# A two-layer hybrid encoder trunk on one core: order of the matmuls in a feature tile, shared PSUM slots, a scan in four parts

## The chip, the cores and the metric

The kernel runs on one core of a Trainium2 chip. The metric is the device time of one execution in microseconds (us), taken as the median of several runs; lower is better. The engines are called TensorE (PE; PEld is its weight load), VectorE (DVE), ScalarE (ACT), GpSimd (POOL) and SyncE (SP), as in the profile.

## The reference, cut to what matters

Two layers work on `x`, 256 tokens of 1024 features, in float32. Each has a token-mixing part and an MLP.

```python
h = rms_norm(x, norm_mix_pre[l])
zq, zk, zv, zx, zy, zxq, zg = in_projection(h, w_in[l])
y_attn = diff_attention(rope(zq), rope(zk), zv, ...)      # 8 heads, two score maps each, chunk-causal
xc = causal_conv(zx, conv_w[l], conv_b[l])
y_lru = rg_lru(xc, ...) * gelu(zy)                        # h_t = a_t * h_(t-1) + u_t along the tokens
y_mem = memory_attention(zxq, mem, ...)                   # 4 heads over 256 memory tokens
merged = gate0 * (y_attn @ w_proj_attn) + gate1 * (y_lru @ w_proj_lru) + gate2 * (y_mem @ w_proj_mem)
x = x + rms_norm(merged @ w_out[l], norm_mix_post[l])
a = relu(rms_norm(x, norm_mlp_pre[l]) @ w_mlp_up[l])
x = x + rms_norm((a * a) @ w_mlp_down[l], norm_mlp_post[l])
```

## The kernel before

**Products in three terms.** Every large product is made from operands split in two parts, a high part (fp32r, the rounded value) and a low part (what is left). The weights come from HBM in chunks of 1 MB (`issue_dma`, three buffers `raw`). `issue_split` (lines 170 to 182) makes of each half chunk a tile `wh` on ScalarE (the cast of line 179) and a tile `wl` on VectorE (the subtraction of line 181); there are five buffers of each, and `weights` (line 184) keeps the splits five halves ahead of their use.

**Feature tiles.** `mm_feat` (line 236) computes 256 output features for all 256 tokens: two halves of 128 features, each in its own PSUM bank of a two-bank slot `acc`. In each half, for each of eight parts k of the contraction, there is one 512-column matmul with `wh` (line 247; its moving operand is two separate blocks of 256 columns, the high and the low part of the activations) and one 256-column matmul with `wl` (line 248), one after the other:

```python
for k in range(8):
    pe.matmul(o.rearrange("p (s n) -> p s n", s=2), wh[:, k, :], av[:, :, k, :], start=(k == 0), stop=False)
    state["mm"] = pe.matmul(o[:, 0:256], wl[:, k, :], av[:, 0, k, :], start=False, stop=(k == 7))
```

Then ScalarE copies one part of the result to SBUF (line 252) and VectorE adds the other (line 253); the sum is the tile `z`. The slot is free after that.

**Token tiles.** `mm_tok` (line 256) makes products with tokens on the partitions, 128 tokens and 512 features to a bank. Both halves of the tokens share one two-bank slot (`acc_tok`, line 121). It uses 512-column matmuls alone (lines 264 to 266). With `apart`, which is set for the last chunk of the second column half of wo and of the down product, all matmuls of token half 0 come ahead of those of half 1. `post_half` and `post_end` (lines 362 and 376) then square the result on ScalarE (line 367, with the sum in `ss4`), multiply it by the gain on VectorE (lines 371 and 387), and add it, scaled, to the residual `xt` (line 388).

**PSUM.** `psacc` has two slots of two banks, `pssc` one slot of two banks for the attention scores (`sc`, line 114), and `psat` two slots of one bank for everything small (`at`).

**Side jobs.** The memory attention (`xattn`), the recurrent branch (`lru`) and the differential attention (`attn`) are generators. `tick`, called in the middle of and after each product tile, moves a job on by one step (`lru` by one step in two ticks), and what the step issues on TensorE is queued behind the last matmul traced so far. `lru` ends with one scan over 2048 columns (line 626) and four steps that make the pair tile `ylr` (lines 631 and 632). `attn` makes in `scores` (line 662) the two score maps of a head in one `sc` tile, whose exponentials (line 680) are the last to read it.

**Order.** The Tile framework places each engine's instructions in an order of its own, by priorities and a time model; each engine then works in order. `tc.high_priority()` brings a block forward. In each layer follow: the memory query product, the recurrent input, the two gates of `lru`, q, k, v, then for each of three branches a gate and a projection (with `attn` beside them, from line 837), then wo, the up product and the down product. In layer 0 memory products for layer 1 stand behind wo and behind the down product; in layer 1 nothing does.

Of the kernel before, what the change touches and what calls it, by code (L numbers as in the profile page):

```python
# [9 lines left out]
F32 = mybir.dt.float32  # L10
# [3 lines left out]
ALU = mybir.AluOpType  # L14
# [54 lines left out]
def trunk(ctx, tc, x_in, xt_in, mem_in, memt_in, w_in, par_in, lamv_in, post_in, rope_in, out):  # L69
    nc = tc.nc  # L70
    act, dve, pe, pool = nc.scalar, nc.vector, nc.tensor, nc.gpsimd
# [4 lines left out]
    p_pair = ctx.enter_context(tc.tile_pool(name="pair", bufs=6))  # L76
    p_tmp = ctx.enter_context(tc.tile_pool(name="tmp", bufs=9))
    p_sm = ctx.enter_context(tc.tile_pool(name="sm", bufs=4))
    ps_acc = ctx.enter_context(tc.tile_pool(name="psacc", bufs=2, space=bass.MemoryType.PSUM))
    ps_sc = ctx.enter_context(tc.tile_pool(name="pssc", bufs=1, space=bass.MemoryType.PSUM))  # L80
    ps_at = ctx.enter_context(tc.tile_pool(name="psat", bufs=2, space=bass.MemoryType.PSUM))

    def pair(name):
# [9 lines left out]
    def hl(t):  # L93

        return t.rearrange("p (s k n) -> p s k n", s=2, k=8)
# [9 lines left out]
    def f8(t):  # L105
        return t.rearrange("p (k n) -> p k n", k=8)

    def tmp(name, dt=F32):
        return p_tmp.tile([128, 512], dt, tag="tmp", name=name)
# [2 lines left out]
        return p_sm.tile([128, n], F32, tag="sm_" + name, name=name)  # L112

    def sc():
        return ps_sc.tile([128, 1024], F32, tag="sc", name="sc")

    def acc():

        return ps_acc.tile([128, 2, 512], F32, tag="acc", name="acc")

    def acc_tok():
        a = acc()
        return [a[:, t, :] for t in range(2)]

# [111 lines left out]
    def mm_feat(key, a):  # L236

        ps = acc()
        av = hl(a)
        for j in range(2):
            wh, wl = (f8(t) for t in weights(*key, j))
            o = ps[:, j, :]
            for k in range(8):
                pe.matmul(o.rearrange("p (s n) -> p s n", s=2), wh[:, k, :], av[:, :, k, :], start=(k == 0), stop=False)  # L247
                state["mm"] = pe.matmul(o[:, 0:256], wl[:, k, :], av[:, 0, k, :], start=False, stop=(k == 7))  # L248
            if j == 0:
                tick()  # L250
        z = tmp("z")
        act.copy(two(z), ps[:, :, 256:512])  # L252
        dve.tensor_tensor(two(z), two(z), ps[:, :, 0:256], op=ALU.add)  # L253
        return z

    def mm_tok(pss, key, a_of, first, last, apart=False):
# [96 lines left out]
    def two(ap):  # L353
        return ap.rearrange("p (i n) -> p i n", i=2)
# [222 lines left out]
    def lru(l, xc, rgw, g2, done):  # L577
        wv = rgw.rearrange("p (c n d) -> p c n d", c=2, n=8)
        xv = f8(xc)
        av, tv = duo("lru")  # L580
        for j in range(4):
            sl = slice(j * 512, (j + 1) * 512)
            ti, xs = tv[:, sl], xc[:, sl]

            def gate(c):
                ps = at()
                for i in range(2):
                    f = 2 * j + i
                    pe.matmul(ps[:, i * 256:(i + 1) * 256], wv[:, c, f, :], xv[:, f, :], start=True, stop=True)
                return ps  # L590

            za, zi = gate(0), gate(1)
            for i in range(2):
                f = 2 * j + i
                act.activation(out=f8(tv)[:, f, :], in_=zi[:, i * 256:(i + 1) * 256], func=AF.Tanh, scale=0.5,
                               bias=hbi[:, l, f:f + 1])
            dve.scalar_tensor_tensor(ti, ti, 1.0, xs, op0=ALU.add, op1=ALU.mult)
            for i in range(2):
                f = 2 * j + i
                dve.tensor_scalar(f8(xc)[:, f, :], za[:, i * 256:(i + 1) * 256], par[:, l, P_BA, f:f + 1], -44.0,  # L600
                                  op0=ALU.add, op1=ALU.max)
            act.activation(out=xs, in_=xs, func=AF.Exp, scale=-1.0)
            yield
        act.activation(out=xc, in_=xc, func=AF.Ln, bias=1.0)
        yield
        for j in range(4):
            sl = slice(j * 512, (j + 1) * 512)
            a, xs = av[:, sl], xc[:, sl]
            act.activation(out=xs, in_=xs, func=AF.Exp, scale=-1.0)
            e = tmp("lE")  # L610
            for i in range(2):
                f = 2 * j + i
                act.activation(out=f8(av)[:, f, :], in_=f8(xc)[:, f, :], func=AF.Exp, scale=ncsp[:, l, f:f + 1])
                act.activation(out=e[:, i * 256:(i + 1) * 256], in_=f8(xc)[:, f, :], func=AF.Tanh,
                               scale=csp[:, l, f:f + 1])
            act.activation(out=xs, in_=a, func=AF.Square)
            dve.scalar_tensor_tensor(xs, xs, 1.0, e, op0=ALU.add, op1=ALU.mult)
            yield
        act.activation(out=xc, in_=xc, func=AF.Sqrt, scale=0.25)
        yield  # L620
        for j in range(4):
            sl = slice(j * 512, (j + 1) * 512)
            dve.tensor_tensor(tv[:, sl], tv[:, sl], xc[:, sl], op=ALU.mult)
        dve.memset(f8(av)[:, :, 0:1], 0.0)
        yield
        dve.tensor_tensor_scan(xc, av, tv, 0.0, op0=ALU.mult, op1=ALU.add)
        yield
        ylr = done["y"] = pair("ylr")
        for j in range(4):
            sl = slice(j * 512, (j + 1) * 512)  # L630
            dve.scalar_tensor_tensor(xc[:, sl], xc[:, sl], 0.5, g2[:, sl], op0=ALU.mult, op1=ALU.mult)
            split_to(hi(ylr)[:, sl], lo(ylr)[:, sl], xc[:, sl])
            yield
# [23 lines left out]
    def attn(l, qT, kT, va, done):  # L657
# [3 lines left out]

        def scores(h):
            pbs[h] = []
            ps = sc().rearrange("p (c n) -> p c n", c=2)
            for b in range(2):
                nk = 128 * (b + 1)
                sv = ps[:, :, 128 * b:128 * b + nk]
                for c in range(2):
                    cs = slice(64 * c, 64 * c + 64)
                    pe.matmul(sv[:, c, :], qv[cs, h, b * 128:(b + 1) * 128], kv[cs, h, 0:nk], start=True, stop=True)  # L670
            for b in range(2):
                nk = 128 * (b + 1)
                sv = ps[:, :, 128 * b:128 * b + nk]
                dve.memset(sv[0:64, :, nk - 64:nk], NEG_BIG)
                nm = sm("anm", 2)
                dve.tensor_reduce(nm, sv, axis=AX.X, op=ALU.max, negate=True)
                e = tmp("ae")
                ss = sm("as", 2)
                for c in range(2):
                    act.activation(out=e[:, c * nk:(c + 1) * nk], in_=sv[:, c, :], func=AF.Exp, bias=nm[:, c:c + 1],  # L680
                                   accum_out=ss[:, c:c + 1])
                r = sm("ar", 2)
                dve.reciprocal(r, ss)
                dve.tensor_scalar(e[:, nk:2 * nk], e[:, nk:2 * nk], r[:, 1:2], lam[:, l:l + 1], op0=ALU.mult,  # L684
                                  op1=ALU.mult)
                dve.scalar_tensor_tensor(e[:, 0:nk], e[:, 0:nk], r[:, 0:1], e[:, nk:2 * nk], op0=ALU.mult,
                                         op1=ALU.subtract)
                pbs[h].append(e)
# [101 lines left out]
    for l in range(DEPTH):  # L790
# [8 lines left out]
        for j in range(4):  # L799
            ps = mm_feat((l, "xq", j), hx)  # L800
            sl = slice(j * 512, (j + 1) * 512)
# [4 lines left out]
        xc, g2 = duo("xcg")  # L806
        for j in range(4):
            ps = mm_feat((l, "x", j), hx)
# [6 lines left out]
        for j in range(4):  # L815
            ps = mm_feat((l, "y", j), hx)
# [6 lines left out]
        for nm, scale, dst, r in (("q", 0.125, qT, rq), ("k", 1.0, kT, rk)):  # L823
            for j in range(4):
                ps = mm_feat((l, nm, j), hx)
# [3 lines left out]
        for n in range(2):  # L829
            pss = acc_tok()  # L830
# [7 lines left out]
        for b, pj, yb in ((2, "pm", {"y": ym}), (1, "pl", ylr), (0, "pa", ya)):  # L838
# [4 lines left out]
            for j in range(4):  # L843
                sl = slice(j * 512, (j + 1) * 512)
                ps = mm_feat((l, "g%d" % b, j), hx)
# [8 lines left out]
                ps = mm_feat((l, pj, j), yb["y"])  # L854
# [11 lines left out]
            mem_gained(l + 1)  # L866
        st = post_begin(l, 0)
        for n in range(2):
            pss = acc_tok()
            for c in range(2):  # L870
                if l + 1 == DEPTH and n == 1 and c == 1:
                    state["ahead"] = 3
                mm_tok(pss, (l, "wo", 2 * n + c), lambda k: parts(mp, 4 * c + k), c == 0, c == 1,
                       n == 1 and c == 1)
            post_half(st, n, pss)
# [16 lines left out]
        for j in range(16):  # L892
            ps = mm_feat((l, "up", j), hx)
# [5 lines left out]
            if j > 0:  # L899
                for i, p in pend:  # L900
# [3 lines left out]
                    sl = slice((i % 4) * 512, (i % 4 + 1) * 512)  # L904
# [1 line left out]
                pend = []  # L906
        st = post_begin(l, 1)
        for n in range(2):
            pss = acc_tok()
            for c in range(8):  # L910

                def a_of(k):
                    f = 4 * c + k
                    return parts(sqs[f // 8], f % 8)

                mm_tok(pss, (l, "dn", 8 * n + c), a_of, c == 0, c == 7, n == 1 and c == 7)
            post_half(st, n, pss)
        post_end(st, pss[1])
    for t in range(2):
        for n in range(2):  # L920
            sl = slice(n * 512, (n + 1) * 512)
# [95 lines left out]
```

## Time and profile before

| | |
|---|---|
| median of 3 runs | 1160.94 us (1160.4 to 1161.4) |
| the profiled execution, its own time | 1162.9 us |
| its span, first to last instruction | 1161.1 us |
| PE busy | 1122.5 us, 97% |
| PEld / DVE / ACT busy | 82% / 74% / 61% |
| mean granted TensorE clock | 0.989 |
| HBM read | 203.02 MB, 176 GB/s over the span |

A row of the trace gives the start and the duration of an instruction, its engine, its line in the kernel, the operation, the tiles it writes and reads, and its shapes; in brackets stands how long the engine was idle before it and what ended that. Matmuls are pipelined: one starts long before the one ahead has ended, so the distance of their starts is the time that each takes of the engine.

### The profile page before, as it was taken

The numbers are of one execution on the slowest core, as the hardware profiler recorded it, in microseconds if no ns is written. First come the engines' busy times: TensorE is split into PE (matmuls) and PEld (weight loads), VectorE is DVE, ScalarE is ACT, GpSimd is POOL, SyncE is SP. The second block draws the span as 40 slices with busy tenths as digits, with TensorE's granted clock in tenths as the row PEclk, the third lists the DMA queues.
The fourth block names the chain that finished last, engine by engine and source line by source line (L and its number), as shares of the span: only waits on it lengthen the run. The fifth ranks groups of instructions, "written<-read, shape, count | busy, mean of one in ns | idle before, by whom it ended". The sixth has DMA issues, their size and how long they took to land. (4 is left out here: it accounts for less than half of the span.)

```text
span 1161.1 us, 15842 instructions
## 1 busy us (share of the span) xinstructions
PE 1122.5 (97%) x6096; PEld 956.6 (82%) x6096; DVE 863.4 (74%) x1347; ACT 705.2 (61%) x1112; POOL 0.7 (0%) x6
## 2 busy tenths in 40 slices
PE   7999999999999999999999999998999997999996
PEld 5789888778888888888888888877788886888885
DVE  6979789778877687774457787987888666887453
ACT  6756695656556566663446667947665554766341
POOL 0000000000000000000000000000000000000000
PEclk9999999989999999999999999999999998999998
DMA  9655346644456545555554534665344553556550
GB/s 326 242 215 181 110 155 207 217 145 146 145 204 214 192 173 185 187 183 205 201 202 167 210 109 145 213 213 179 122 146 167 212 183 109 187 199 213 181 181 37
DMA packets 34779, 209.28 MB, mean 180 GB/s; under 512 B 3856, under 2 KB 8080, under 8 KB 10768
## 3 DMA queue, kind: packets, MB, share of 16 engines
q1 hardware_dynamic: 34128, 206.18, 50.5%
q10 hardware_dynamic: 576, 2.10, 0.5%
q8 instruction: 48, 0.79, 0.3%
q14 instruction: 27, 0.22, 0.1%
HBM read 203.02 MB, written 1.05 MB: 176 GB/s over the span
## 5 line engine op out<-in xcount | busy, mean ns | idle before, releaser
L181 DVE TENSOR_TENSOR wl<-raw,wh 128x1024 fp32r<-128x1024 f32 (+1 forms) x369 | 449.1, 1220 | 216.1 <-ACT wh L179 215.0
L179 ACT CAST wh<-raw 128x1024 fp32r<-128x1024 f32 (+1 forms) x369 | 385.0, 1048 | 325.8 <-PE acc L247 166.5
L247 PE MATMUL acc<-hx,wh 128*128 128x512 f32 x1536 | 550.3, 401 | 6.5 <-ACT vmg L835 2.9
L248 PE MATMUL acc<-hx,wl 128*128 128x256 f32 x1536 | 432.9, 282 | 0.0
L247 PEld LDWEIGHTS acc<-hx,wh 128*128 128x128 f32 x1536 | 290.1, 189 | 77.4 <-ACT vmg L835 3.7
L248 PEld LDWEIGHTS acc<-hx,wl 128*128 128x128 f32 x1536 | 292.0, 190 | 2.5 <-issue 2.0
L266 PE MATMUL acc<-wh,sq 128*128 128x512 f32 x256 | 99.6, 389 | 0.0
L265 PE MATMUL acc<-wl,sq 128*128 128x512 f32 x256 | 99.6, 389 | 0.0
L264 PE MATMUL acc<-wh,sq 128*128 128x512 f32 x256 | 99.6, 389 | 0.0
L253 DVE TENSOR_TENSOR z<-z,acc 128x512 f32<-128x512 f32 x128 | 87.1, 681 | 8.7 <-ACT z L252 8.7
L252 ACT COPY z<-acc 128x512 f32<-128x512 f32 x128 | 74.3, 580 | 9.5 <-PE acc L248 9.4
L265 PEld LDWEIGHTS acc<-wl,sq 128*128 128x128 f32 x256 | 48.1, 188 | 10.0
L264 PEld LDWEIGHTS acc<-wh,sq 128*128 128x128 f32 x256 | 48.1, 188 | 10.0
L266 PEld LDWEIGHTS acc<-wh,sq 128*128 128x128 f32 x256 | 48.1, 188 | 9.9
L247 PE MATMUL acc<-mh,wh 128*128 128x512 f32 x128 | 47.7, 412 | 6.9 <-ACT wh L179 6.9
L247 PE MATMUL acc<-xq,wh 128*128 128x512 f32 x128 | 46.5, 401 | 1.1 <-ACT wh L179 1.1
L247 PE MATMUL acc<-ylr,wh 128*128 128x512 f32 x128 | 46.0, 401 | 0.5 <-DVE z L253 0.5
L247 PE MATMUL acc<-ya,wh 128*128 128x512 f32 x128 | 45.6, 399 | 0.0
L248 PE MATMUL acc<-mh,wl 128*128 128x256 f32 x128 | 36.9, 288 | 1.2 <-DVE wl L181 1.2
L248 PE MATMUL acc<-xq,wl 128*128 128x256 f32 x128 | 36.5, 285 | 1.5 <-DVE wl L181 1.5
L248 PE MATMUL acc<-ya,wl 128*128 128x256 f32 x128 | 36.0, 281 | 0.0
L248 PE MATMUL acc<-ylr,wl 128*128 128x256 f32 x128 | 35.8, 280 | 0.0
(202 smaller groups left out, 1407.2 us busy)
## 6 DMA issues: line engine op xcount, KB each, us to landing
raw<-in_w SPq DMA_DIRECT2D x183, 1024.0 KB, 4.8
qkT<-rqk SPq DMA_DIRECT2D x32, 128.0 KB, 4.4
rgw<-in_w SPq DMA_DIRECT2D x2, 1024.0 KB, 7.0
post<-in_post ACTq DMA_DIRECT2D x4, 512.0 KB, 4.1
mem<-in_memt SPq DMA_DIRECT2D x4, 256.0 KB, 4.6
memr<-in_mem SPq DMA_DIRECT2D x2, 512.0 KB, 7.1
xt<-in_x SPq DMA_DIRECT2D x2, 512.0 KB, 10.2
xf<-in_xt SPq DMA_DIRECT2D x1, 1024.0 KB, 12.1
```

What stands on the lines that cost most here:

```text
L179: act.copy(h[:, sl], r[:, sl])
L181: dve.tensor_tensor(l[:, sl], r[:, sl], h[:, sl].bitcast(F32), op=ALU.subtract)
L247: pe.matmul(o.rearrange("p (s n) -> p s n", s=2), wh[:, k, :], av[:, :, k, :], start=(k == 0), stop=False)
L248: state["mm"] = pe.matmul(o[:, 0:256], wl[:, k, :], av[:, 0, k, :], start=False, stop=(k == 7))
L252: act.copy(two(z), ps[:, :, 256:512])
L253: dve.tensor_tensor(two(z), two(z), ps[:, :, 0:256], op=ALU.add)
L264: pe.matmul(pss[t], ah[:, sl], wh[:, k, :], start=(first and half == 0 and k == 0), stop=False)
L265: pe.matmul(pss[t], ah[:, sl], wl[:, k, :], start=False, stop=False)
L266: m = pe.matmul(pss[t], al[:, sl], wh[:, k, :], start=False, stop=(last and half == 1 and k == 1))
```

## The change

In `mm_feat` the eight 512-column matmuls of a half come first, then its eight 256-column ones, and the copy and the addition that make `z` get priority. The pool of scores is gone: `psacc` has three two-bank slots, which feature tiles, token tiles and score tiles share. For the second column half of wo and of the down product each half of the tokens gets a slot of its own (one bank of it is used). The scan of `lru` is done in four parts of 512 columns, over two steps of the job in place of one.

```diff
-    ps_acc = ctx.enter_context(tc.tile_pool(name="psacc", bufs=2, space=bass.MemoryType.PSUM))
-    ps_sc = ctx.enter_context(tc.tile_pool(name="pssc", bufs=1, space=bass.MemoryType.PSUM))
+    ps_acc = ctx.enter_context(tc.tile_pool(name="psacc", bufs=3, space=bass.MemoryType.PSUM))
...
     def sc():
-        return ps_sc.tile([128, 1024], F32, tag="sc", name="sc")
+        return ps_acc.tile([128, 2, 512], F32, tag="acc", name="sc")
...
-    def acc_tok():
+    def acc_tok(apart=False):
+        if apart:
+            return [acc()[:, 0, :] for t in range(2)]
         a = acc()
         return [a[:, t, :] for t in range(2)]
...
             for k in range(8):
                 pe.matmul(o.rearrange("p (s n) -> p s n", s=2), wh[:, k, :], av[:, :, k, :], start=(k == 0), stop=False)
+            for k in range(8):
                 state["mm"] = pe.matmul(o[:, 0:256], wl[:, k, :], av[:, 0, k, :], start=False, stop=(k == 7))
...
         z = tmp("z")
-        act.copy(two(z), ps[:, :, 256:512])
-        dve.tensor_tensor(two(z), two(z), ps[:, :, 0:256], op=ALU.add)
+        with tc.high_priority():
+            act.copy(two(z), ps[:, :, 256:512])
+            dve.tensor_tensor(two(z), two(z), ps[:, :, 0:256], op=ALU.add)
...
-        dve.tensor_tensor_scan(xc, av, tv, 0.0, op0=ALU.mult, op1=ALU.add)
-        yield
+        for j in range(4):
+            sl = slice(j * 512, (j + 1) * 512)
+            dve.tensor_tensor_scan(xc[:, sl], av[:, sl], tv[:, sl], 0.0, op0=ALU.mult, op1=ALU.add)
+            if j % 2:
+                yield
...
-            ps = sc().rearrange("p (c n) -> p c n", c=2)
+            ps = sc()
...
         for n in range(2):
-            pss = acc_tok()
+            pss = acc_tok(n == 1)
```

The last of these edits is made twice, for wo and for the down product.

## Rows read from the trace of the kernel before

**Rows 1.** The page: totals of the engines; the chain that ended last, by engine

```profile
PE 1122.5 (97%) x6096; PEld 956.6 (82%) x6096; DVE 863.4 (74%) x1347; ACT 705.2 (61%) x1112; POOL 0.7 (0%) x6
...
PE 27%; DVE 3%; ACT 1%; issue 0%; DVEq 0%; ACTq 0%
```

**Rows 2.** Windows, line 247: us, PE, PEld busy (count), PEclk, DMA share, GB/s

```profile
0.00:1161.10 1161.10, 735.03 (x2048) 386.81 (x2048) 0.99 0.51 180
```

**Rows 3.** Timeline of PE, layer 1's up product: first and last of 208 starts

```profile
990.22 0.39 PE L247 MATMUL acc<-hx,wh 128*128 128x512 f32 x1
...
1061.98 0.39 PE L247 MATMUL acc<-hx,wh 128*128 128x512 f32 x1
```

**Rows 4.** Timeline of PE, layer 0's up product: first and last of 204 starts

```profile
442.01 0.40 PE L247 MATMUL acc<-hx,wh 128*128 128x512 f32 x1
...
513.73 0.40 PE L247 MATMUL acc<-hx,wh 128*128 128x512 f32 x1
```

**Rows 5.** Windows, line 264, layer 1's down product (columns as in group 2)

```profile
1070.00:1150.00 80.00, 45.79 (x118) 22.06 (x118) 1.00 0.41 145
```

**Rows 6.** Timeline of PE: twelve 256-column matmuls of the memory scores, and the next

```profile
83.79 1.60 PE L507 MATMUL at<-ka,xq 128*128 128x256 f32 x12
85.23 0.40 PE L247 MATMUL acc<-hx,wh 128*128 128x512 f32 x1
```

**Rows 7.** Waits: who for whom, total us, times, longest us

```profile
PE at L318 <- DVE xt L388: 5.3, 2, 3.9
PE sc L670 <- ACT ae L680: 4.0, 2, 2.0
PE acc L247 <- DVE z L253: 3.1, 6, 0.7
...
PE acc L248 <- DVE wl L181: 2.8, 4, 0.8
```

**Rows 8.** Timeline of PE, layer 0, from v into the attention stretch

```profile
214.22 0.50 PE L247 MATMUL acc<-hx,wh 128*128 128x512 f32 x1 [1.43 <-ACT vmg L835]
217.24 0.93 PE L670 MATMUL sc<-qkT 64*128 64x128 f32 x8
221.71 0.49 PE L247 MATMUL acc<-xq,wh 128*128 128x512 f32 x1 [0.53 <-ACT wh L179]
...
244.78 0.93 PE L670 MATMUL sc<-qkT 64*128 64x128 f32 x8 [1.99 <-ACT ae L680]
```

**Rows 9.** Timeline of ACT in the same stretch

```profile
213.10 2.06 ACT L835 COPY vmg<-acc 128x512 f32<-128x512 f32 x4 [0.76 <-DVE ylr L231]
...
227.22 0.58 ACT L252 COPY z<-acc 128x512 f32<-128x512 f32 x1
```

**Rows 10.** Windows: us, PE, PEld, DVE, ACT, POOL busy (x), PEclk, DMA share, GB/s

```profile
225.00:240.00 15.00, 14.85 (x92) 12.20 (x92) 14.08 (x28) 10.05 (x23) 0.00 (x0) 1.00 0.81 281
240.00:250.00 10.00, 7.39 (x35) 5.90 (x35) 7.21 (x18) 5.90 (x18) 0.00 (x0) 0.78 0.30 106
```

**Rows 11.** The scan in layer 0 (timeline of DVE), and the window around it

```profile
194.98 4.42 DVE L626 TENSOR_TENSOR_SCAN xcg<-lru 128x2048 f32<-128x2048 f32 x1
...
130.00:200.00 70.00, 70.00 (x387) 60.78 (x386) 61.13 (x86) 55.38 (x79) 0.00 (x0) 1.00 0.54 181
```

**Rows 12.** Timelines of PE, ACT and DVE at the end of the kernel

```profile
1151.26 0.39 PE L266 MATMUL acc<-wh,sq 128*128 128x512 f32 x1
...
1151.69 0.60 ACT L367 ACTIVATE junk<-acc 128x512 f32<-128x512 f32 x1 [12.54 <-PE acc L266]
...
1153.86 1.42 DVE L388 SCALAR_TENSOR_TENSOR xt<-post,ry,xt 128x512 f32<-128x512 f32 x2
...
1156.63 1.42 DVE L388 SCALAR_TENSOR_TENSOR xt<-post,ry,xt 128x512 f32<-128x512 f32 x2
```

**Rows 13.** Timeline of DVE behind layer 1's wo

```profile
966.88 1.41 DVE L388 SCALAR_TENSOR_TENSOR xt<-post,ry,xt 128x512 f32<-128x512 f32 x2
...
968.98 1.41 DVE L388 SCALAR_TENSOR_TENSOR xt<-post,ry,xt 128x512 f32<-128x512 f32 x2
```

More of the change, by code (lines that the diff above doesn't have):

```diff
@@ L908, in trunk @@
         for n in range(2):
-            pss = acc_tok()
+            pss = acc_tok(n == 1)
             for c in range(8):
```

## The prediction

> **What bounds the kernel now.** I read the page's totals first, then the waits of TensorE (PE), then its matmuls in order of time, then the chains at the two ends of a token-major product. PE is busy for 97% of the span, and the chain that ended last is almost only PE work [rows 1]. So what counts is how fast matmuls follow one another, and the few places where PE stands.
>
> Busy time does not show the first. A feature tile is made of pairs: a 512-column matmul with a part of wh, then a 256-column one with the same part of wl, in all 2048 pairs [rows 2]. In layer 1's up product the 512-column matmuls start at 990.22 and, 207 pairs later, at 1061.98 us: 346.7 ns a pair [rows 3]. In layer 0's, the same code, from 442.01 to 513.73 us, 203 pairs: 353.3 ns [rows 4]. PE is "busy" throughout in both. There are two levels, 6.6 ns apart. I take half to six tenths of all pairs to be at the slow one: an estimate, from looking through the stretches without waits, which hold one of the two levels each; [rows 3, 4] are the longest of either.
>
> Where only one kind follows itself there is one level. In 80 us of layer 1's down product line 264 starts 118 times, and it is every third of the 512-column matmuls there: 80 / 354 = 226 ns each [rows 5]. Twelve of 256 columns, 83.79 to 85.23 us: 120 ns [rows 6]. The sum, 346 ns, is the fast level.
>
> Next PE's waits, the longest in total but for the casts that the start waits for: 5.3 us for xt, 4.0 for a free score tile, 3.1 for z, 2.8 for wl [rows 7], and in layer 0 1.43 for v's copies [rows 8]; layer 1 is the same code, so I count it twice, 2.9.
>
> **The change, part by part.** The sum is made against the profiled execution: span 1161.1, its own time 1162.9 us, which is 2.0 above the median of 1160.9. What is saved inside the span I take off the median.
>
> *Grouping.* No matmul is added or taken away; their order within each half tile changes. Then 7 of 8 gaps are between equals, so I take the fast level for all. Saved: 2048 x 0.55 x 6.6 ns = 7.4 us. What the trace does not show is the 512-column matmul of two separate 256-column parts following itself. Its lower bound is 226 ns (one contiguous part [rows 5]). Its upper bound is what the slow level [rows 4] leaves it if the partner takes no more than its 256 columns at 2.4 GHz, 353.3 - 106.7 = 247 ns: then a pair takes 367, 17 ns over today's mean of 350, a loss of 35 us. I take the lower one, since the fast level already holds that very matmul within 346.7 ns, with 120 left for its partner; the price is nearest to [rows 5].
> The Trainium skill (TensorE: Matmul & The Clock Gate, "Back-to-back issue gap") gives columns / 2.4 GHz + 2.5 ns per matmul: 215.8 + 109.2 = 325 ns a pair. By that the grouped pairs would save 2048 x 25 = 51 us. The trace does not agree: the 226 ns of [rows 5] are 10 ns above it in a run with nothing between.
>
> *wl later.* The first use of a wl moves back by seven 512-column matmuls, 1.6 us, past the longest wait for one, 0.8 us [rows 7]. I take off 2.0 of the 2.8 us of these waits. The wh is also free earlier, the wl not later.
>
> *z first.* In the attention stretch the tile that ended before 221.71 has its copy z at 227.22, over five us later [rows 8, 9], behind casts. With priority it goes ahead of them. What is moved back is a cast by 0.58 and a subtraction by 0.68 us; halves are split five ahead, 2.8 us each, which hides it. Without that cover it would be 0.6 us per tile. z's wait goes from 3.1 to about 0.6: 2.5 us.
>
> *Three shared slots.* Feature tiles get a third slot where no scores run. The wait for v's copies (a tile waits for v's slot) should go, as the next tile takes the third slot. But the copies wait for ylr's last subtraction [rows 9], and the scan in two steps moves ylr's four steps back by two ticks of some 2.7 us. With the third slot the copies may come 5.6 us (one tile) later; so I count only half, 1.5 us. (ScalarE works in order: casts behind a copy that waits are held up too, and have five halves of cover. No DMA is moved, on any queue.) In attention, scores had one slot, and PE stood 1.99 us for the exponentials at 244.78 [rows 8], in each layer alike (4.0 us in 2 waits [rows 7]); in layer 0 the granted clock then averaged 0.78 over ten microseconds, part of it at 1.2 GHz [rows 10]. I take 3.0 of the 4.0 us and 1.5 us of clock. I don't take more, because VectorE is busy for 14.08 of 15 us there [rows 10]: another slot lets work pile up but makes none of it faster.
>
> *Scan in four.* 4.42 us once per layer [rows 11]; four parts cost as much plus three starts, from nothing to a whole 512-column operation each, 0.7 us (1.41 for two [rows 13]). PE is busy 70.00 of the 70 us around it [rows 11], with z and splits ahead of it. Nothing, beyond the step above; 2.1 us a layer if that cover is gone.
>
> *Two slots for the second half of wo and down.* At the end of the kernel the last matmul starts at 1151.26; ScalarE, idle for 12.54 us, starts the square of token half 0 only at 1151.69, though that half's matmuls were through 2.7 us (12 x 226.5 ns) earlier: it waited for the tile. Half 0's xt starts at 1153.86, half 1's at 1156.63 [rows 12]. With a slot each, half 0 is worked off beside half 1's matmuls, and half 1 takes half 0's place: xt from 1153.86 in place of 1156.63, 2.8 us less. After layer 1's wo the same shape stands ahead of the transposes, which wait 5.3 us for xt [rows 7]. Half 1's xt can start where half 0's does, 966.88 in place of 968.98 [rows 13]: 2.1 us less, between 0 (hx's splits last anyway) and 4 (with the wait of half 0's transposes gone as well). In layer 0 the memory products stand behind both ends, and nothing is counted.
>
> Sum: 7.4 + 2.0 + 2.5 + 1.5 + 3.0 + 1.5 + 2.8 + 2.1 = 22.8. With some 2 us for new waits in the attention stretch: 1160.9 - 20.8 = **1140 us**.
>
> **The rivals.**
> *R1, the pairs stay as they are.* If the two levels come from something else than the alternation, and grouped matmuls fall into them as well, 7.4 us are lost from the sum: 1147. For it: same code, two levels. Against: [rows 5, 6] hold one rate. With the upper bound of 247 ns in a third of the tiles it is 1159.
> *R2, the shared slots turn against it: slower.* In attention feature tiles and score tiles now take turns in three slots; a period of both is about 7 us (two halves of 2.8, a score group of 0.93 and transposes), so 21 us of slot time. A score tile is held from 217.24 to its last exponential, which ends ahead of the copy at 227.22 [rows 8, 9], 10 us; a feature tile from 214.22 to that copy and the addition, 14 us. Together 24: 3 us a period are missing, and PE would stand about as long for each head as it does now for one, 1.99 us. That is 16 x 2 = 32 us; less the 12 us that slots don't touch (7.4 + 2.8 + 2.1): 1160.9 + 32 - 12 = 1181. It decides from the point where z no longer comes within about 5 us of its last matmul. With priority z comes in 2, so the tile is held 8, and 18 is under 21: against it.
> The Trainium skill (same page, "A second HAM failure mode: psum-queue depth-cycling") says that short idles between groups which cycle through PSUM banks make the clock swing. Products that cycle through two slots for 70 us keep 1.00 [rows 11], so the trace bears this out only where PE stands, as at 240 us; it would add to R2's price, not make one of its own.
> *R3, the gap vanishes.* 768 columns at 2.4 GHz are 320 ns; without any gap 2048 x 30 = 61 us go, and with the other 13 us 1086 comes out. No row comes near it; the page's gap would be most of it.
>
> **How the numbers follow.** Forecast 0.70, its own range 1132 to 1147. R1 0.20 (nearly all of it still faster). R2 0.08, of which half ends above the old time, the rest only eats the gain. R3 0.02. The range must hold 8 in 10: from 1130 (all of the waits of [rows 7] and v's, 18 us, with 7.4, 2.8 and the clock's 1.5 to 2.5) to 1152 (R1 with a few of its dearer tiles, or the mild half of R2). A measurement of this kernel can tell about 0.2%, 2.3 us. Faster by more: 0.70 + 0.17 of R1 + 0.03 of R2 + 0.02 = 0.92; the same 0.02 + 0.01 = 0.03; slower 0.01 + 0.04 = 0.05.
>
> **What would show it.** Right: one rate in all up products, 512-column starts 226 to 227 ns apart and 256-column ones 120; the square of half 0 under the last twelve matmuls, and xt's last half within about 3.6 us of the last matmul; no PE wait for scores' exponentials of 1.99 us; z's copy within 1 us of its last matmul. Wrong: 512-column starts 236 to 240 ns apart when grouped; PE waiting for "ae" or z oftener than 2 and 6 times; a clock under 1.00 between 200 and 300 us for longer than before; v's copies more than 6 us behind v's last matmul.

## The result, and the profile after

The change takes 1144.45 us (median of 4 runs, 1141.38 to 1145.87) against 1161.14 for the kernel before on the same chip: a ratio of 0.9854, with an interval of 0.9831 to 0.9876. A second set of runs gave 1143.85 and 0.9837 (0.9815 to 0.9858). Predicted were 1140 us, with a range of 1130 to 1152.

| | before | after |
|---|---|---|
| profiled execution, its own time | 1162.9 us | 1145.87 us |
| its span | 1161.1 us | 1144.1 us |
| PE waits in all, from the full list of waits | 28.7 us | 20.3 us |
| time lost to the clock: sum over windows of 20 us, up to the last matmul, of length x (1 - granted clock) | 8.6 us | 8.8 us |
| mean granted clock | 0.989 | 0.991 |

The page of the change, its totals and the chain that ended last, answers to [rows 1]:

```profile
PE 1117.0 (98%) x6096; PEld 961.1 (84%) x6096; DVE 862.7 (75%) x1353; ACT 705.0 (62%) x1112; POOL 0.7 (0%) x6
...
PE 97%; ACT 1%; DVE 1%; DMA 0%; issue 0%; SPq 0%; DVEq 0%
```

The number of matmuls is the same, and PE is 97% of the chain. (The row of before covers only 31% of the span, 27 of them PE [rows 1]; the prediction's "almost only PE work" says more than that row does.) The 17.0 us of span came out of the rate and out of the places where PE stands. The longest waits of PE in the change (who for whom, total us, times, longest us) answer to [rows 7]:

```profile
PE acc L248 <- ACT wh L180: 10.4, 3, 6.2
PE sc L676 <- ACT ae L686: 3.3, 2, 1.6
PE at L321 <- DVE xt L391: 2.9, 2, 2.6
```

The waits for z, for wl and for v's copies are gone, and that for xt went from 5.3 to 2.9 us. Those for hx and mh, the split operands at the start of a product, grew from 0.7 to 3.7 us in all. The wait for scores fell only from 4.0 to 3.3. The first line is new in part: 6.2 us of it are the start, as before, but the other 4.2 are two waits for a cast, one in each layer.

**The rate.** PE in the up products of the change, layer 0 (to the first matmul of the down product), then layer 1; "x8" is a row of eight, whose first start is given. These answer to [rows 3, 4]:

```profile
436.88 2.00 PE L248 MATMUL acc<-hx,wh 128*128 128x512 f32 x8
...
503.92 0.40 PE L267 MATMUL acc<-wh,sq 128*128 128x512 f32 x1
...
977.50 2.00 PE L248 MATMUL acc<-hx,wh 128*128 128x512 f32 x8
...
1044.54 2.00 PE L248 MATMUL acc<-hx,wh 128*128 128x512 f32 x8
```

The windows of line 248 there count them (us, PE, PEld busy with count, PEclk, DMA share, GB/s). The first also counts one matmul that started at 435.70, the second also the eight from 974.61 and seven behind 1044.54; so 192 pairs lie in the 67.04 us of either.

```profile
436.00:503.00 67.00, 48.03 (x193) 34.53 (x192) 1.00 0.54 189
974.00:1047.00 73.00, 52.18 (x208) 37.41 (x208) 1.00 0.56 198
```

67.04 / 192 = 349.2 ns a pair in both layers, where 353.3 and 346.7 stood [rows 4, 3]. Layer 0 gained; **layer 1 lost**. In these stretches there is one rate now, and it is not the fast one. Within a half tile of layer 1, and in one that follows a product made of 512-column matmuls alone, PE shows why:

```profile
389.71 1.98 PE L248 MATMUL acc<-mh,wh 128*128 128x512 f32 x8
391.53 0.28 PE L250 MATMUL acc<-mh,wl 128*128 128x256 f32 x1
...
991.47 2.00 PE L248 MATMUL acc<-hx,wh 128*128 128x512 f32 x8
993.31 1.12 PE L250 MATMUL acc<-hx,wl 128*128 128x256 f32 x8
994.26 0.40 PE L248 MATMUL acc<-hx,wh 128*128 128x512 f32 x1
```

Behind 512-column matmuls, eight of line 248 take 391.53 - 389.71 = 1.82 us, 227 ns each, the rate of [rows 5]. Behind 256-column ones they take 993.31 - 991.47 = 1.84, and the eight of 256 columns 0.95, that is 119 ns each. The second is a little under the rate of [rows 6], the first over that of [rows 5].

What this is worth over the whole kernel can be added up from the starts in the traces. Take each feature matmul whose next matmul on PE is a feature matmul too and starts without a wait, leave out the first 20 us and the stretches at the lower clock, and add the mean distance of a 512-column matmul to its next start and that of a 256-column one. This gives 354.9 ns a pair before and 353.1 in the change: **1.8 ns, or 3.7 us over 2048 pairs**. Both lie above the rates of the up products; which pairs elsewhere cost more was not followed up. The same sums show that a wait costs PE some 0.2 us beyond the idle time in the list, 2.3 us at 13 such places before and 0.3 at 2 in the change.

**The new wait.** ScalarE in layer 0, around the end of `lru` and of v, answers to [rows 9]; in brackets the idle time before a row and what ended it:

```profile
196.51 1.06 ACT L180 CAST wh<-raw 128x1024 fp32r<-128x1024 f32 x1 [1.66 <-PE acc L269]
...
202.82 1.83 ACT L231 CAST ylr<-xcg 128x512 fp32r<-128x512 f32 x3 [5.26 <-DVE xcg L637]
...
207.88 1.07 ACT L841 COPY vmg<-acc 128x512 f32<-128x512 f32 x2 [0.81 <-DVE ylr L232]
210.11 1.07 ACT L841 COPY vmg<-acc 128x512 f32<-128x512 f32 x2 [1.16 <-PE acc L269]
211.07 5.79 ACT L180 CAST wh<-raw 128x1024 fp32r<-128x1024 f32 x6
...
222.43 0.57 ACT L255 COPY z<-acc 128x512 f32<-128x512 f32 x1
```

Between 196.51 and 211.07 ScalarE makes no `wh` at all, though it is idle for 5.26 us ahead of the casts of `ylr`, and then six in a row. PE runs out of them, in layer 0 and in layer 1; a third row is the end of the tile whose z the last row above copies:

```profile
212.18 2.11 PE L248 MATMUL acc<-hx,wh 128*128 128x512 f32 x8 [2.11 <-ACT wh L180]
...
217.97 1.11 PE L250 MATMUL acc<-hx,wl 128*128 128x256 f32 x8
...
770.85 2.50 PE L248 MATMUL acc<-hx,wh 128*128 128x512 f32 x5 [2.11 <-ACT wh L180]
```

The Trainium skill (PSUM — Partial Sum Buffer, "Engine vs sequencer instructions") says that ScalarE's queue is strictly first in, first out. The trace is in line with it: the casts held up behind the copies come only at 211.07, six of them without a gap.

**The end of the kernel** answers to [rows 12] (timelines of PE, ACT and DVE):

```profile
1136.97 0.39 PE L269 MATMUL acc<-wh,sq 128*128 128x512 f32 x1
...
1134.67 0.60 ACT L370 ACTIVATE junk<-acc 128x512 f32<-128x512 f32 x1 [9.83 <-PE acc L269]
...
1137.39 0.60 ACT L370 ACTIVATE junk<-acc 128x512 f32<-128x512 f32 x1 [1.60 <-PE acc L269]
...
1136.84 1.42 DVE L391 SCALAR_TENSOR_TENSOR xt<-post,ry,xt 128x512 f32<-128x512 f32 x2
...
1139.62 1.41 DVE L391 SCALAR_TENSOR_TENSOR xt<-post,ry,xt 128x512 f32<-128x512 f32 x2
```

The square of token half 0 runs 2.3 us ahead of the last matmul's start, and the last xt starts 1139.62 - 1136.97 = 2.65 us behind it, where it was 1156.63 - 1151.26 = 5.37.

### The profile page after: what moved, and what is told of

Read it like the earlier page. It is cut to its first block, busy times and chain, and to the rows that moved or that the text cites. A ratio compares the mean times of both kernels' runs of the same rounds, so it can differ in the third digit from the quotient of the medians.

```text
span 1144.1 us, 15861 instructions
## 1 busy us (share of the span) xinstructions
PE 1117.0 (98%) x6096; PEld 961.1 (84%) x6096; DVE 862.7 (75%) x1353; ACT 705.0 (62%) x1112; POOL 0.7 (0%) x6
## 4 chain that ended last, share of the span: by engine, by line
PE 97%; ACT 1%; DVE 1%; DMA 0%; issue 0%; SPq 0%; DVEq 0%
PE acc L248 42%; PE acc L250 21%; PE acc L267 9%; PE acc L268 9%; PE acc L269 9%; PE at L592 1%; PE sc L676 1%; PE at L545 1%; PE at L510 1%; PE at L711 1%; PE at L321 1%; ACT wh L180 0%; DMA raw<-in_w 0%; PE at L726 0%; PE at L530 0%
## 5 line engine op out<-in xcount | busy, mean ns | idle before, releaser
L248 PE MATMUL acc<-hx,wh 128*128 128x512 f32 x1536 | 394.9, 398 | 5.5 <-ACT wh L180 4.2
L250 PEld LDWEIGHTS acc<-hx,wl 128*128 128x128 f32 x1536 | 209.6, 190 | 15.3
L250 PE MATMUL acc<-hx,wl 128*128 128x256 f32 x1536 | 214.3, 282 | 0.0
L269 PEld LDWEIGHTS acc<-wh,sq 128*128 128x128 f32 x256 | 48.1, 188 | 10.1
L248 PE MATMUL acc<-mh,wh 128*128 128x512 f32 x128 | 35.1, 414 | 7.9 <-ACT wh L180 6.2
L248 PEld LDWEIGHTS acc<-mh,wh 128*128 128x128 f32 x128 | 23.9, 195 | 13.4 <-ACT wh L180 6.2
L248 PE MATMUL acc<-ylr,wh 128*128 128x512 f32 x128 | 32.6, 396 | 0.0
L686 ACT ACTIVATE ae<-sc,anm 128x128 f32<-128x128 f32 (+1 forms) x64 | 26.7, 420 | 8.9 <-DVE anm L682 8.7
L248 PE MATMUL acc<-ya,wh 128*128 128x512 f32 x128 | 32.1, 392 | 0.0
L248 PEld LDWEIGHTS acc<-xq,wh 128*128 128x128 f32 x128 | 24.1, 199 | 6.3 <-issue 2.0
L855 ACT ACTIVATE th<-z,hbg 128x256 f32<-128x256 f32 x48 | 22.0, 502 | 7.5 <-DVE z L256 7.3
```

Of the source, the lines that this page charges most:

```text
L269: m = pe.matmul(pss[t], al[:, sl], wh[:, k, :], start=False, stop=(last and half == 1 and k == 1))
L855: act.activation(out=th[:, i * 256:(i + 1) * 256], in_=ps[:, i * 256:(i + 1) * 256], func=AF.Tanh, scale=0.5, bias=hbg[:, l, b, f:f + 1])
```

## The experiments

All times are medians. Each ratio is to the kernel before on the same chip, whose median was 1161.1 to 1162.9 us in the different sets.

### g_only: the kernel before with the grouping alone

```diff
             for k in range(8):
                 pe.matmul(o.rearrange("p (s n) -> p s n", s=2), wh[:, k, :], av[:, :, k, :], start=(k == 0), stop=False)
+            for k in range(8):
                 state["mm"] = pe.matmul(o[:, 0:256], wl[:, k, :], av[:, 0, k, :], start=False, stop=(k == 7))
```

> The kernel before with the grouping of the matmuls alone. The trace of the changed kernel shows that a 512-column matmul which follows a run of 256-column ones is slow for about five matmuls (233, 236, 228, 233, 231 ns), then 226.7; a run of 256 starts faster (113 to 119) and settles at 120. Theory A (a toll per change of kind): each of the 256 half tiles costs about 20 ns over the fast level, so pairs take 349 to 350 ns in both layers alike, where they took 346.7 or 353.3; that gains some 3 us over all pairs, and the waits for wl (2.8 us) go: 1155 to 1156 us against 1161. Rival B (my prediction): 7.4 us of pairs and 2 of wl, 1151 to 1152. Rival C (order of no effect by itself, all came from slots and priority): within 1.5 us of 1161.

Measured: 1155.84 us, 0.9947 (0.9927 to 0.9968), 5.6 us less than before. Two of its waits of PE:

```profile
PE acc L247 <- DVE z L254: 6.6, 6, 1.6
...
PE acc L265 <- ACT wh L179: 2.3, 1, 2.3
```

The wait for wl is gone (2.8) and those for v's copies and for scores are 1.7 us shorter each, but that for z is 3.5 us longer and that for a cast at the first token product 2.3 in place of 1.2; in all PE waits 28.0 us here, 28.7 before. By the sums above a pair costs 353.5 ns in place of 354.9, 2.8 us. Theory A's time and its term for the pairs came out; its waits did not, for they gave 0.7 us and not 2.8. The grouping alone is worth about a third of the change.

### g_undo: the change with the pairs again

```diff
-            for k in range(8):
                 state["mm"] = pe.matmul(o[:, 0:256], wl[:, k, :], av[:, 0, k, :], start=False, stop=(k == 7))
```

> The changed kernel with its matmuls back in pairs; slots, priority and scan as in the change. Theory A: 4 to 6 us slower than the change, 1148 to 1151 us, with two levels of 346.7 and 353.3 ns a pair again and waits for wl again. Rival B: 8 to 10 us slower, 1152 to 1155. Rival C: the same as the change, 1143 to 1146.

Measured: 1142.84 us, 0.9838 (0.9815 to 0.9861): not slower than the change. Part of it is the rate. PE in the up products of this kernel, layer 0, then layer 1:

```profile
440.83 0.39 PE L248 MATMUL acc<-hx,wh 128*128 128x512 f32 x1
...
500.11 0.39 PE L248 MATMUL acc<-hx,wh 128*128 128x512 f32 x1
...
983.14 0.40 PE L248 MATMUL acc<-hx,wh 128*128 128x512 f32 x1
...
1043.20 0.40 PE L248 MATMUL acc<-hx,wh 128*128 128x512 f32 x1
```

Its windows of line 248 (the second also counts the start at 982.78):

```profile
441.00:500.00 59.00, 59.00 (x171) 31.80 (x171) 1.00 0.53 189
983.00:1043.00 60.00, 60.00 (x171) 31.95 (x170) 1.00 0.54 188
```

59.28 / 171 = 346.7 ns in layer 0, 60.06 / 170 = 353.3 in layer 1. The two levels are those of before, but **the layers have changed places**. So which level a stretch of pairs falls into differs from build to build, and isn't fixed by the layer. The other part is the cast: here one of `wh` stands between the first two of `ylr`, though the scan is in four parts, and PE doesn't wait at the end of v.

```profile
204.73 0.62 ACT L231 CAST ylr<-xcg 128x512 fp32r<-128x512 f32 x1 [2.48 <-DVE xcg L636]
205.26 1.05 ACT L180 CAST wh<-raw 128x1024 fp32r<-128x1024 f32 x1
207.07 0.62 ACT L231 CAST ylr<-xcg 128x512 fp32r<-128x512 f32 x1 [0.76 <-DVE xcg L636]
```

Over all stretches a pair costs 355.0 ns here and 353.1 in the change, so the pairs do lose 3.8 us; but PE waits 15.9 us in place of 20.3, and the clock loses 3.4 us in place of 8.8. The time falls in the range of rival C, or just under it, without its reason. So the two edits aren't a sum of their own gains: ScalarE's order differs from kernel to kernel.

### scan_one: the change with the scan in one part

```diff
-        for j in range(4):
-            sl = slice(j * 512, (j + 1) * 512)
-            dve.tensor_tensor_scan(xc[:, sl], av[:, sl], tv[:, sl], 0.0, op0=ALU.mult, op1=ALU.add)
-            if j % 2:
-                yield
+        dve.tensor_tensor_scan(xc, av, tv, 0.0, op0=ALU.mult, op1=ALU.add)
+        yield
```

> The changed kernel with the scan in one part and in one step of its job, as before. Theory A (the extra step makes ylr's casts and the copies of v late on ScalarE, the casts of wh queue behind them, and PE waits 2.1 us for a cast in each layer, after which the clock may fall): the wait for wh of 2.1 us at the start of the first gate goes or shrinks under 1 us in each layer, and the kernel gains 2 to 5 us over the change, 1139 to 1142. Rival D (the wait comes from the order that the framework gives ScalarE, whatever the scan's steps): PE waits 1.4 to 2.3 us there as before, the time is within 1.5 us of the change, 1143 to 1146. Rival E (one long scan blocks VectorE for 4.4 us with z behind it): slower by 1 to 3 us, with new waits around the scan.

Measured: **1139.47 us**, 0.9811 (0.9788 to 0.9833), 5.0 us faster than the change. ScalarE in the same stretch:

```profile
196.64 1.05 ACT L180 CAST wh<-raw 128x1024 fp32r<-128x1024 f32 x1 [1.67 <-PE acc L269]
200.53 0.62 ACT L231 CAST ylr<-xcg 128x512 fp32r<-128x512 f32 x1 [2.84 <-DVE xcg L634]
201.06 2.13 ACT L180 CAST wh<-raw 128x1024 fp32r<-128x1024 f32 x2
204.01 0.62 ACT L231 CAST ylr<-xcg 128x512 fp32r<-128x512 f32 x1 [0.82 <-DVE xcg L634]
```

Two casts stand between those of `ylr`, and PE goes from v (last start 209.81 us) into the next tile without a wait:

```profile
210.04 1.98 PE L248 MATMUL acc<-hx,wh 128*128 128x512 f32 x8
```

The clock follows. The window behind the end of v in layer 1, first of the change, then of this kernel (busy us of PE, PEld, DVE, ACT, POOL, then PEclk, DMA share, GB/s):

```profile
770.00:780.00 10.00, 9.15 (x44) 7.51 (x45) 8.16 (x12) 8.47 (x12) 0.00 (x0) 0.83 0.58 210
```

```profile
770.00:780.00 10.00, 9.10 (x52) 7.63 (x51) 6.86 (x12) 8.52 (x16) 0.00 (x0) 1.00 0.28 99
```

In the change the clock is at 1.2 GHz for part of the stretch behind PE's wait of 2.11 us (770.85), and again (0.83 from 790 to 800 us) behind one of 1.64 us for scores at 793.51; here it stays at 2.4 GHz in both windows. The same sums as in the table above give 17.8 us of waits (2.5 less) and 3.4 us of clock (5.4 less). Together that is 7.9, more than the 6.3 us between the two spans, so the clock's sum is rough here. Executions at one clock point the same way: at a mean of 0.995 the change's fastest took 1141.38 us and four of scan_one 1138.8 to 1140.9, so what is left there is about the size of the waits.

### scan_4_1step: the change with four scan parts in one step

```diff
             dve.tensor_tensor_scan(xc[:, sl], av[:, sl], tv[:, sl], 0.0, op0=ALU.mult, op1=ALU.add)
-            if j % 2:
-                yield
+        yield
```

> The changed kernel with the scan in four parts, but in one step of its job, so that the steps behind it come no later than before. It tells which half of the scan edit costs the 5 us that scan_one gained. Theory L (the extra step): as scan_one, 1138 to 1141 us, no wait of 2 us for a cast at the first gate. Theory M (the parts: four short operations let the framework bring ylr's casts together and the casts of wh behind them): as the change, 1143 to 1146 us, with that wait in both layers.

Measured: 1145.34 us, 0.9853 (0.983 to 0.9877), the time of the change. ScalarE:

```profile
200.02 0.62 ACT L231 CAST ylr<-xcg 128x512 fp32r<-128x512 f32 x1 [2.97 <-DVE xcg L636]
203.50 1.83 ACT L231 CAST ylr<-xcg 128x512 fp32r<-128x512 f32 x3 [2.85 <-DVE xcg L636]
```

Again no cast of `wh` stands between them, and PE waits 2.11 us at 211.66. So it is not the second step of the job but the four parts, by the order that they lead to on ScalarE, and they lead to it in the grouped kernel: g_undo has the same four parts without that wait.

### undo_one: scan_one with the pairs again

The edit is that of g_undo, made to scan_one.

> The changed kernel with the scan in one part (as in scan_one, 1139.5 us) and the matmuls in pairs again. In the run with pairs and the scan in four, the pairs lost 3.8 us, but the wait for wh casts behind v was gone and the time was not worse. Here neither has that wait, so the toll can be seen by itself. Theory A (toll per change of kind, 349.7 ns a pair against a mix of 346.7 and 353.3, and waits for wl): 3 to 6 us slower than scan_one, 1142.5 to 1145.5. Rival G (the order of the matmuls matters only through the order that the framework then gives the other engines): 1138 to 1141.

Measured: 1149.6 us, 0.9902 (0.9884 to 0.992), 10.1 us slower than scan_one. Here both layers' up products are at the slow level (from 440.81 to 500.18 us 168 pairs, from 985.14 to 1040.26 156: 353.4 and 353.3 ns), and wl is waited for:

```profile
PE acc L267 <- DVE wl L182: 3.7, 2, 1.8
...
PE acc L249 <- DVE wl L182: 2.7, 4, 0.8
```

Neither expectation held. The profiled spans are 9.1 us apart. By the sums over all stretches a pair costs 355.5 ns here and 353.0 in scan_one, 5.0 us; PE waits 19.6 us in place of 17.8 (6.4 more for wl, but 0.3 in place of 4.1 for scores); and the clock loses 5.2 us in place of 3.4. That is 8.6.

Side by side, the four kernels that have the other edits in common (times in us; g_undo and undo_one have pairs):

| | scan in four parts | scan in one |
|---|---|---|
| grouped | 1144.45 (the change) | 1139.47 (scan_one) |
| pairs | 1142.84 (g_undo) | 1149.60 (undo_one) |

**The two edits act on each other.** With groups the scan in four parts costs 5.0 us; with pairs it gains 6.8. The grouping brings nothing with four parts and 10 us with one, though the pairs themselves always cost 2.8 to 5.0 us more than the groups (this and the comparisons above); the rest is waits and clock.

### whole_one: scan_one, both halves' 512-column matmuls ahead of both halves' 256-column ones

```diff
+        w = []
         for j in range(2):
-            wh, wl = (f8(t) for t in weights(*key, j))
+            w.append([f8(t) for t in weights(*key, j)])
...
+        for j in range(2):
+            o = ps[:, j, :]
+            for k in range(8):
+                state["mm"] = pe.matmul(o[:, 0:256], w[j][1][:, k, :], av[:, 0, k, :], start=False, stop=(k == 7))
```

> scan_one with grouping over the whole tile: sixteen 512-column matmuls, then sixteen 256-column ones, so half as many changes of kind (128 in place of 256). Theory A (the toll belongs to the change of kind): a pair takes about 348.2 ns in place of 349.7, some 2.5 us less in all, 1136 to 1138. Rival H (the toll belongs to the half tile, its bank or its weights): 349.7 ns a pair, time as scan_one, 1138.5 to 1140.5, or slower by waits for wh, since two halves are held at once.

Measured: 1142.17 us, 0.9834 (0.9817 to 0.9852), 2.7 us slower than scan_one. PE in layer 1's up product:

```profile
985.18 3.82 PE L249 MATMUL acc<-hx,wh 128*128 128x512 f32 x16
988.84 2.08 PE L256 MATMUL acc<-hx,wl 128*128 128x256 f32 x16
990.75 3.82 PE L249 MATMUL acc<-hx,wh 128*128 128x512 f32 x16
```

Sixteen 512-column matmuls take 3.66 us, 0.03 over 16 x 226.7 ns, as much as the eight above are over theirs: the excess comes once per run, not with each matmul. A pair costs 5.57 / 16 = 348.1 ns. But a tile now holds two halves of the splits, PE waits 2.9 us for wl (1.4 at the longest), and the little that the rate gives is more than lost: theory A's rate came out, its time did not. In all PE waits 19.9 us, 2.1 more than in scan_one; where the rest of the 2.7 us lies is not settled.

### z_plain_one: scan_one without the priority for z

```diff
-        with tc.high_priority():
-            act.copy(two(z), ps[:, :, 256:512])
-            dve.tensor_tensor(two(z), two(z), ps[:, :, 0:256], op=ALU.add)
+        act.copy(two(z), ps[:, :, 256:512])
+        dve.tensor_tensor(two(z), two(z), ps[:, :, 0:256], op=ALU.add)
```

> scan_one without the priority for z. Theory J (shared slots need an early z: a feature tile held 14 us and a score tile held 10 do not fit three slots at a period of 7): new waits of PE for z or for the exponentials in both attention stretches, 3 us or more in each, 1144 to 1152 us. Rival I (the third slot by itself is enough, z may be late): 1138.5 to 1140.5 us, no wait for z over 1 us.

Measured: 1141.86 us, 0.9831 (0.9814 to 0.9849), 2.4 us over scan_one, with the wait back and that for scores shorter (2.3 us in place of 4.1):

```profile
PE acc L248 <- DVE z L255: 3.4, 4, 1.1
```

The time lies between the two expectations: z's priority is worth something beside the third slot, but far less than theory J said.

### tok_shared and tok_one: the token halves in one slot again

Made to the change (tok_shared) and to scan_one (tok_one), for wo and for the down product:

```diff
-            pss = acc_tok(n == 1)
+            pss = acc_tok()
```

> The changed kernel with both halves of the tokens in one slot again for wo and the down product. Theory A: the end is 2.7 us later (xt's last half starts 5.4 us after the last matmul in place of 2.7), and PE's wait for xt behind layer 1's wo goes from 2.9 back to 5.3 us: 4 to 6 us slower than the change, 1148 to 1151. Rival F (behind wo the splits of hx decide): only the end is later, 1147.

> scan_one with both token halves in one slot again: what the two slots are worth where no wait for casts is about. Theory A: 2.7 us at the end and 2.4 us of PE's wait for xt behind layer 1's wo, 1143.5 to 1146 us against 1139.5. Rival F (only the end): 1141.5 to 1142.8.

Measured: 1147.78 us, 0.9882 (0.986 to 0.9904), 3.3 us over the change; and 1144.34 us, 0.9838 (0.9818 to 0.9859), 4.9 us over scan_one. PE waits for xt as before the change, 5.4 and 5.5 us, that is 2.5 and 2.6 more. But it waits 1.3 and 1.4 us less for hx, so behind layer 1's wo less than that is lost: the 193rd matmul of the up product starts 46.7 us after wo's last matmul in both, and 44.6 and 44.7 us after it in the change and in scan_one, 2.1 and 2.0 less. With 2.7 at the end that makes 4.7 to 4.8, about theory A's size. Beside scan_one it is what was measured; beside the change the executions of the two kernels spread over 4 us each and overlap.

### own_one: scan_one with scores in a slot of their own and token halves in one

```diff
-    ps_acc = ctx.enter_context(tc.tile_pool(name="psacc", bufs=3, space=bass.MemoryType.PSUM))
+    ps_acc = ctx.enter_context(tc.tile_pool(name="psacc", bufs=2, space=bass.MemoryType.PSUM))
+    ps_sc = ctx.enter_context(tc.tile_pool(name="pssc", bufs=1, space=bass.MemoryType.PSUM))
...
-        return ps_acc.tile([128, 2, 512], F32, tag="acc", name="sc")
+        return ps_sc.tile([128, 2, 512], F32, tag="sc", name="sc")
...
-            pss = acc_tok(n == 1)
+            pss = acc_tok()
```

> scan_one with the slots as before the change: two for tiles, one for scores, and both token halves in one slot. The token halves alone are worth 3.3 us by the earlier run (1147.8 against 1144.4), so 1142.8 would stand if the third slot were worth nothing. Theory J: waits for z (6.6 us in the run with grouping alone) and for the copies of v come back, 1148 to 1153 us. Rival K (priority for z does it all): 1142 to 1144.5 us.

Measured: 1150.62 us, 0.9907 (0.989 to 0.9924), 11.1 us over scan_one. Without the 4.9 of tok_one, some 6 us are left for the third slot, as theory J had it in time, though the wait for z is 2.0 us and not 6.6. The waits name only part of that, these two for z and 0.8 us for v's copies:

```profile
PE acc L249 <- DVE z L257: 1.0, 2, 0.5
PE acc L268 <- DVE z L257: 1.0, 1, 1.0
```

The wait for scores is about the same with a slot of their own (3.8 us) as with three shared (4.1). What PE gains by the third slot is feature tiles that needn't wait for z and v; it isn't room for scores. The profiled executions are 9.3 us apart: 2.7 at the end and 4.1 in PE's waits (21.9 in all); the other 2.5 stay open.

### change_again: the change once more, beside scan_4_1step and tok_one

> The changed kernel itself, beside the two others on one chip. All theories: 1141 to 1146 us; the spread goes with the granted clock, since the waits of 2 us are followed by a stretch at 1.2 GHz in some executions and not in others.

Measured: 1143.85 us, 0.9837 (0.9815 to 0.9858), with the wait of 2.11 us at 211.26 again. The four runs of either set spread with the clock: 1141.38 us at a mean granted clock of 0.995, 1145.87 at 0.991.

## Why the prediction was right, and where its terms were not

The total came out 4.4 us over the forecast, inside the range. That is in part luck, since terms that were too large stood against gains that were not counted. Its steps, in their order:

- **Grouping, 7.4 us: the term that was mis-sized.** The forecast took the fast level of 346.7 ns for all pairs. The grouped pairs go at 349.2 in both layers, between the two levels. With the forecast's own share at the slow level, the mean before would be 350.3, and only 2048 x 1.1 ns = 2.3 us would be left. Counted over all stretches it is 1.8 ns, 3.7 us (and 2.8, 3.8 and 5.0 us in g_only, g_undo and undo_one, each beside its grouped or paired partner): half of the forecast, since the pairs before also stood above the level that was taken for them. The bound "one contiguous part [rows 5]" for the 512-column matmul was right, for behind others of its kind it takes 227 ns. What was missing is the price of each change of kind. By the upper bound of 247 ns nothing happened. R1, that grouped matmuls fall into two levels as well, is wrong as it stood; its price, that nothing is gained here, was about as far off as the forecast's.
- **The page's formula** (the Trainium skill, TensorE: Matmul & The Clock Gate, "Back-to-back issue gap"), which that section gives for an isolated matmul, made 215.8 and 109.2 ns. Also in groups the trace shows 227 and 119, so the measurement decides against it here, and R3 is gone.
- **wl later, 2.0 us.** Right: all 2.8 us of that wait are gone.
- **z first, 2.5 us.** Right in size: z_plain_one costs 2.4. Wrong in one detail, for the copy was to come within 1 us of the last matmul. The tile that ends by 219.1 us has its copy at 222.43, over 3 us later, behind exponentials and two casts (219.51 and 221.02 us); before, it was over five [rows 8, 9].
- **v's copies, 1.5 us: wrong sign.** The wait for the copies, 2.9 us in all, is gone, but two of 2.11 us for a cast stand in its place. The forecast had seen that casts behind the copies are held up and that "five halves of cover" hide it, and had put "2.1 us a layer if that cover is gone" beside the scan. The cover, at some 2.8 us each about 14, is just what runs out between 196.51 and 211.07. The agreement in size is chance, since that 2.1 was three starts of a scan part. Scan_one and scan_4_1step show the cause: four parts, through ScalarE's order; g_undo shows that it takes the grouping as well.
- **Scores, 3.0 us, and clock, 1.5 us: mis-sized.** The wait fell by 0.7. The doubt stated there, that another slot makes none of the work faster, is borne out by own_one: with a slot of their own scores wait 3.8 us, with three shared ones 4.1. The clock gave nothing (8.6 us lost before, 8.8 after): over windows of 20 us it was 0.91 in place of 0.83 in layer 0's attention stretch, but 0.91 over 40 us (760 to 800) in layer 1's, where it had been 1.00.
- **The end, 2.8 us, and layer 1's wo, 2.1 us.** Right: 2.7, and 2.0 to 2.1 by tok_shared and tok_one, where 2.4 us less of waiting for xt bring 1.3 more for hx.
- **"Some 2 us for new waits in the attention stretch".** They came, 4.2 us, but at its start, behind v, and not from the slots.

Summed up for the profiled execution: waits 8.4, what waits cost beyond their idle time 2.0, pairs 3.7, end 2.7, clock -0.2, which is 16.6 of 17.0 us of span. The waits include 0.3 us less at the start of the kernel, which no edit touched, and the clock's share is rough.

R2, the shared slots turning against the kernel, did not come: PE waits twice for exponentials, never for z. R3's 61 us were nowhere near.

The forecast of 1140 was reached by a kernel that is not the change: scan_one, the change without the four scan parts, at 1139.47 us is the best version of this study and beats both kernels.

## What to carry to other kernels

When matmuls are grouped by size, count the changes of kind as well as the rate within a group, and read a pair's cost in several stretches of the old kernel, since the same pairs can stand at two levels from build to build. An edit that only splits one engine's operation can change the order that the framework gives to another engine, and do so in one build and not in the next; so look at what the in-order engine does in its idle time ahead of a late operand, and at how long the buffers made ahead of it last. Test each part of a bundle alone and taken out of the whole: here the scan in four parts cost 5 us with groups and gained 7 with pairs, and the grouping was worth nothing or 10 us, depending on the rest.

## What the runs showed of the hardware that was not expected

- **A change of kind and back costs about 20 ns.** Eight 512-column matmuls behind 256-column ones take about 27 ns more than eight at 226.7, and eight 256-column ones behind 512-column ones about 10 less than at 120. It doesn't depend on the operand of two parts: the token product behind 256-column matmuls starts at 503.92, 504.15, 504.39, 504.62, 504.85 and 505.08 us, 232 ns apart, and has 227 from then on (505.08 to 510.07 us, 22 matmuls).
- **Alternating pairs have two levels, 346.7 and 353.3 ns,** and which stretch gets which differs between builds of the same code: slow and fast in the two layers before, fast and slow in g_undo, slow and slow in undo_one. What decides it stays open.
- **A wait of about 2 us can cost clock afterwards, or not.** Behind 2.11 us in layer 0 of the change the clock stayed at 1.00 (from 205 to 230 us), behind the same 2.11 us in layer 1 the mean was 0.83 over ten microseconds. In tok_shared, with the same two waits, it was the other way round: 0.83 from 210 to 220 us, 1.00 from 770 to 780. The change's own executions differ by 4.5 us at mean clocks of 0.995 and 0.991, and 0.004 of 1144 us is 4.6; behind which waits the faster one kept its clock, no trace shows.
